# The attention queries of a macaron block as a sixth Strassen group, with queries, keys and values parked in DRAM

## The chip, the core and the metric

The kernel runs on one core of a Trainium2 chip. The metric is the device time of one launch in microseconds, the median of three runs. One further execution was taken with the hardware profiler; all rows below come from it. Engines are named as in the profile: PE (matmuls), PEld (weight loads), DVE (VectorE), ACT (ScalarE), POOL (GpSimd), SP (the queue that starts most loads).

## What is computed

One block on x of 256 tokens by 2048 channels, float32: a half-step SwiGLU feed-forward, then a mixer stage, then a second half-step feed-forward and a last RMSNorm. The mixer stage, which the change touches:

```
h = rmsnorm(x, norm_mix_g)
q_a, k_a, v_a, q_r, k_r, v_r, g_r, gate_a, gate_r = split(h @ w_in)   # widths 1024 x 7, 2048 x 2
att = chunked_band_attention(q_a, k_a, v_a, rel_bias)    # 8 heads of 128, softmax(q k^T + bias) v
ret = silu(g_r) * chunkwise_retention(rotary(q_r), rotary(k_r), v_r)
merged = sigmoid(gate_a) * (att @ w_out_att) + sigmoid(gate_r) * (ret @ w_out_ret)
x = x + merged @ w_out
```

## The kernel before

**Products in three parts.** Every float32 weight chunk of 256 x 512 (KC = 2 blocks of 128 rows) is split into hi and lo: ACT casts it (`hi`, L129), DVE subtracts (`lo`, L130). Each product then takes three matmuls (`three`: hi·hi L140, lo·hi L141, hi·lo L143).

**Steps.** The program is one list of steps, made before anything is issued; `run` walks it. A *standard* step is one chunk against both token tiles: 12 matmuls. A *Strassen group* takes two column blocks of 512 and both token tiles and makes seven half-size products where plain multiplication has eight. It is 28 substeps of 6 matmuls in four phases: phase 0, 1 and 2 have eight each (four r, four s, written 0 to 3), phase 3 has four s. Four "kept" chunks k and four x chunks of the group live in SBUF through the phases. Phase 0 adds k to x (`first`, L532, a DVE add). Phase 1 adds the raw chunk to x (L594), and `third` makes k = x - k (L580) and starts an accumulating DMA on x from POOL (L581). For the chunks named in `added`, the add of phase 0 is an accumulating DMA too (`add_on`, L547), which POOL starts once x has landed; the feed-forwards use `ADDED = (2, 3)`, the gates of the mixers before use none.

**Where standard steps go.** `weave` makes the mixer list: 8 standard steps first (MIX_LEAD), then the groups, with standard steps set between pairs of substeps by a credit that MIX_SHARE gives per pair (four pairs in each of the phases 0 to 2, four single substeps in phase 3). Before, the groups are four gate pairs (`gates`, sigmoid) and the retention gate (silu), five in all, named by their first step: z392, z430, z467, z505, z543. Seven standard jobs of eight steps are woven in: qa0, qa1, ka0, ka1, va0, va1, vr0. `mixed` is the step where the list of groups ends; then come vr1, qr0, kr0, qr1, kr1 as standard jobs (40 steps), and the merge from `mixed + 40`.

**How far engines run ahead.** `prep_upto(c + 4)` splits up to four chunks ahead of the step on PE (SPLIT_BUFS = 4). Raw chunks come by SP's queue through five buffers (RAW_BUFS). k and x of the next group come by POOL's queue, eight at a time (KEPT); where `weave` gets `extra`, ten. All large tiles share one pool of 30 (ACT_TILES). Work called with `later(n, fn)` is issued n steps on, behind the splits of that step, so it stands in line on each engine.

**Attention.** `att_qk_done` scales a finished q or k block, PE transposes it, ACT and DVE copy one half each into a tile (`to_transposed`, L842, L844). From `mixed + 4` on, each head takes five stages, offsets 0, 1, 2, 4, 6 (scores, exp, shares, transposes, values), a new head every four steps. Its PSUM tiles come from a ring of two ("side"), which the transposes of qr and kr and the retention scores also use.

Of the kernel before, what the change touches and what calls it, by code (L numbers as in the profile page):

```python
# [8 lines left out]
F32 = mybir.dt.float32  # L9
F32R = mybir.dt.float32r  # L10
AF = mybir.ActivationFunctionType
# [4 lines left out]
P = 128  # L16
SEQ = 256
NT = SEQ // P
# [3 lines left out]
HEADS = 8  # L22
# [4 lines left out]
NB = 512  # L27
# [7 lines left out]
EXTRA = 2  # L35
# [5 lines left out]
MIX_LEAD = 8  # L41
RET_WAIT = (14, 5)
HELD = 6

MIX_SHARE = (0.85,) * 4 + (1.0,) * 4 + (0.8,) + (0.4,) * 3 + (0.15,) * 4
SHARE = (0.75,) * 4 + (1.0,) * 4 + (0.0,) * 4 + (0.2,) * 4
ADDED = (2, 3)
PLAIN = 10
# [27 lines left out]
def block_kernel(ctx: ExitStack, tc: tile.TileContext, x, g1, w1g, w1u, w1d, gm, w_in, rel, woa, wor, wo,  # L76
                 g2, w2g, w2u, w2d, gf, cos, sin, decay, ident, out):
    nc = tc.nc
# [8 lines left out]
    dram = ctx.enter_context(tc.tile_pool(name="dram", bufs=1, space=bass.MemoryType.DRAM))  # L87

    def act_tile(dt, name):
        return apool.tile([P, 4, SEQ], dt, tag="act", name=name)  # L90
# [7 lines left out]
    def tmp_tile(name, tag="t", bufs=None):  # L98
        return tmp.tile([P, NB], F32, tag=tag, name=name, bufs=bufs)


    steps = []
# [6 lines left out]
    def later(n, fn):  # L109
        due.setdefault(state["step"] + n, []).append(fn)  # L110
# [109 lines left out]
    def add(jobs):  # L220
        for job in jobs:
            for k in range(0, job.nk, KC):
                steps.append(standard(job, k))
# [83 lines left out]
    table = {}  # L307
# [507 lines left out]
    nm = Norm("nm", gains[:, 1, :], True)  # L815
# [11 lines left out]
    QA, KA, VA, QR, KR, VR, GR, GA, GG = 0, W, 2 * W, 3 * W, 4 * W, 5 * W, 6 * W, 7 * W, 7 * W + D  # L827
    scale = HD ** -0.5
    tposed, nat = {}, {}

    def heads_t(ts):
        return slice(ts * P, (ts + 1) * P)

    def to_transposed(key, b, srcs, steps):

        dst = act_tile(F32, f"{key}{b}T")
        tposed[key, b] = dst

        def go(t):
            ps = transpose4(srcs[t], f"{key}{b}p{t}").rearrange("p (i q) -> p i q", i=4)  # L840
            if t == 0:
                nc.scalar.copy(dst[:, :, heads_t(t)], ps)  # L842
            else:
                nc.vector.tensor_copy(dst[:, :, heads_t(t)], ps)  # L844

        for t in range(NT):
            later(steps[t], lambda t=t: go(t))

    def att_qk_done(key, b):
        def done(acc):  # L850
            srcs = []
            for t in range(NT):
                s = tmp_tile(f"{key}{b}{t}", "qk", 4)
                nc.scalar.activation(s, acc[t], AF.Copy, scale=nm.scale(t))
                srcs.append(s)
            to_transposed(key, b, srcs, (2, 2))

        return done
# [32 lines left out]
    def nat_done(key, b, func, after=None):  # L891
        def done(acc):
            dst = act_tile(F32, f"{key}{b}")
            nat[key, b] = dst.rearrange("p a q -> p (a q)").rearrange("p (t n) -> p t n", t=NT)
            for t in range(NT):
                nc.scalar.activation(nat[key, b][:, t, :], acc[t], func, scale=nm.scale(t))
            if after is not None:
                after()

        return done  # L900
# [63 lines left out]
    def all_attention():  # L964
        for h in range(HEADS):
            for s, stage in attention(h):
                later(2 + 4 * h + s, stage)

    def retention(b):

# [53 lines left out]
    w_in0 = w_in[0]  # L1024

    def proj(col, done, tags=("acc", "z")):
        return Gemm(w_in0, 0, col, D // P, nm, done, tags)
# [8 lines left out]
    def gates(col1, col2, func, dsts):  # L1036


        def evict(t, side, r):
            if side == 1:  # L1040
                nc.scalar.activation(r, r, func)
            else:
                bank, r = r, tmp_tile(f"sg{col1}{t}", "gate", 2)
                nc.scalar.activation(r, bank, func, scale=nm.scale(t))
            nc.scalar.dma_start(dsts[side][:, t, :], r)

        return Strassen(nm, w_in0, col1, w_in0, col2, evict)

    both = ("acc", "acc")
    groups = {  # L1050
        b: (lambda b=b: gates(GA + b * NB, GG + b * NB, AF.Sigmoid, merge_dram[b])) for b in range(D // NB)
    }
    groups["gr"] = lambda: gates(GR, GR + NB, AF.Silu, ret_dram)
    weave(
        [proj(QA + b * NB, att_qk_done("qa", b), both) for b in range(2)]
        + [proj(KA + b * NB, att_qk_done("ka", b), both) for b in range(2)]
        + [proj(VA + b * NB, nat_done("va", b, AF.Copy), both) for b in range(2)]
        + [proj(VR, nat_done("vr", 0, AF.Copy), both)],
        0, groups, MIX_LEAD, MIX_SHARE,
    )  # L1060
    mixed = len(steps)
    add([proj(VR + NB, nat_done("vr", 1, AF.Copy))])
    for b in range(2):
        add([proj(QR + b * NB, ret_qk_done("qr", b)), proj(KR + b * NB, ret_qk_done("kr", b, lambda b=b: retention(b)))])

# [79 lines left out]
    def at(step, fn):  # L1145
        due.setdefault(step, []).append(fn)
# [52 lines left out]
    at(mix - 18, load_rel)  # L1199
    at(mix - 18, lambda: later(4, load_gain(gm, 1)))  # L1200
    at(mixed - 4, set_bias)
    at(mixed + 2, all_attention)
    at(merges[0][0] + 4, lambda: later(8, load_gain(g2, 2)))
    at(mixed + 16, load_ret_gates)
    at(mixed + 20, set_decay)
# [66 lines left out]
```

## Time and profile before

| | us |
|---|---|
| median of three runs | 2061.39 (2060.89 to 2062.56) |
| the profiled execution | 2061.97 |
| its span (first to last instruction) | 2060.1 |
| PE busy | 2037.8, 99% of the span |
| DVE busy | 1766.2, 86% |
| ACT busy | 1494.1, 73% |

The span is what the profiler sees; the run's time is 1.9 us longer. The list of all idle time on PE comes to some 22 us, about 5 us of which is the start. The first feed-forward takes the span to about 680, the mixer groups stand from about 708 to 1050, attention and retention to about 1160, the merge to about 1370, the second feed-forward to the end. Busy time of an engine is given by the instructions' own durations; on DVE these overlap a little where one starts before the other has drained.

### The profile page before, as it was taken

What the parts mean: (1) busy time and instruction counts of PE and PEld (TensorE: products, weight loads), DVE (VectorE), ACT (ScalarE), POOL (GpSimd) and SP (SyncE); (2) the same over time, 40 slices, a digit from 0 to 9 for tenths busy, and PEclk for the clock granted to TensorE, in tenths of its full rate; (3) what the DMA queues carried; (4) which work ended last, traced back from release to release, by engine and by line L of the source; (5) the groups of instructions that cost most, each with busy time, mean ns of one, the idle gap of its engine ahead of it and who ended that gap; (6) DMA issues with size and microseconds to landing.
All of it is one profiled execution on the core that took longest, in us unless ns stands there. A gap on an engine that the chain in (4) does not pass through costs nothing.

```text
span 2060.1 us, 26318 instructions
## 1 busy us (share of the span) xinstructions
PE 2037.8 (99%) x9208; PEld 1685.6 (82%) x9208; DVE 1766.2 (86%) x1836; ACT 1494.1 (73%) x1892; POOL 344.8 (17%) x386
## 2 busy tenths in 40 slices
PE   9999999999999999999999999999999999999998
PEld 7888888888888888888888888888888888888886
DVE  7999999999999799889966667569989999989996
ACT  8778877887877767776765434556788888887875
POOL 2221222221222110121100000012122212112200
PEclk9999999999999999999999999999999999999999
DMA  9888899888888677898786645578889888889983
GB/s 308 252 232 260 252 274 273 254 229 252 254 250 244 241 206 262 263 288 240 228 277 184 216 142 189 185 231 218 267 267 278 255 255 234 269 261 268 276 214 133
DMA packets 230325, 498.47 MB, mean 242 GB/s; under 512 B 15584, under 2 KB 16336, under 8 KB 230192
## 3 DMA queue, kind: packets, MB, share of 16 engines
q1 hardware_dynamic: 156736, 301.50, 43.5%
q0 software_dynamic: 70112, 189.44, 36.0%
q10 hardware_dynamic: 3344, 5.84, 0.8%
q8 instruction: 72, 1.18, 0.2%
q14 instruction: 61, 0.50, 0.1%
HBM read 487.81 MB, written 8.91 MB: 241 GB/s over the span
## 4 chain that ended last, share of the span: by engine, by line
PE 92%; ACT 3%; DVE 3%; issue 1%; DMA 1%; DVEq 0%; ACTq 0%; POOLq 0%; POOL 0%
PE acc L143 15%; PE acc L140 15%; PE acc L141 15%; DVE lo L130 1%; DMA raw<-in_w_in_dram 1%; ACT hi L129 0%; PE z392a L143 0%; PE z873a L140 0%; PE z910a L141 0%; PE z765a L141 0%; PE z543a L143 0%; PE z430a L143 0%; PE z801a L143 0%; PE z392a L141 0%; PE z505a L143 0%
## 5 line engine op out<-in xcount | busy, mean ns | idle before, releaser
L130 DVE TENSOR_TENSOR lo<-raw,hi 128x1024 fp32r<-128x1024 f32 x367 | 447.1, 1221 | 142.6 <-ACT hi L129 140.8
L129 ACT CAST hi<-raw 128x1024 fp32r<-128x1024 f32 x367 | 384.3, 1051 | 173.3 <-PE acc L141 138.0
L794 ACT ACTIVATE xall<-acc 128x512 f32<-128x512 f32 x160 | 94.5, 591 | 14.5 <-PE acc L143 10.3
L791 ACT ACTIVATE acc<-xall 128x512 f32<-128x512 f32 x160 | 95.8, 599 | 8.2 <-DVE f1g L758 4.3
L140 PE MATMUL acc<-hi,mgh 128*128 128x512 f32 x128 | 50.2, 392 | 0.0
L141 PE MATMUL acc<-hi,mgl 128*128 128x512 f32 x128 | 49.8, 389 | 0.0
L140 PE MATMUL acc<-hi,nma01h 128*128 128x512 f32 x96 | 38.8, 404 | 0.1
L140 PE MATMUL acc<-hi,nma00h 128*128 128x512 f32 x96 | 38.6, 402 | 0.0
L141 PE MATMUL acc<-hi,nma00l 128*128 128x512 f32 x96 | 37.5, 390 | 0.0
L141 PE MATMUL acc<-hi,nma01l 128*128 128x512 f32 x96 | 37.5, 390 | 0.0
L140 PE MATMUL acc<-hi,nma10h 128*128 128x512 f32 x96 | 37.5, 390 | 0.0
L141 PE MATMUL acc<-hi,nma11l 128*128 128x512 f32 x96 | 37.4, 390 | 0.0
L140 PE MATMUL acc<-hi,nma11h 128*128 128x512 f32 x96 | 37.4, 390 | 0.0
L141 PE MATMUL acc<-hi,nma10l 128*128 128x512 f32 x96 | 37.4, 390 | 0.0
L143 PE MATMUL acc<-lo,mgh 128*128 128x512 f32 x128 | 35.5, 389 | 0.0
L143 PE MATMUL acc<-lo,nma01h 128*128 128x512 f32 x96 | 29.6, 390 | 0.0
L143 PE MATMUL acc<-lo,nma11h 128*128 128x512 f32 x96 | 29.6, 389 | 0.0
L143 PE MATMUL acc<-lo,nma00h 128*128 128x512 f32 x96 | 29.6, 389 | 0.0
L143 PE MATMUL acc<-lo,nma10h 128*128 128x512 f32 x96 | 29.6, 389 | 0.0
L143 PEld LDWEIGHTS acc<-lo,mgh 128*128 128x128 f32 x128 | 24.0, 188 | 5.0
L141 PEld LDWEIGHTS acc<-hi,mgl 128*128 128x128 f32 x128 | 24.0, 188 | 4.9
L140 PEld LDWEIGHTS acc<-hi,mgh 128*128 128x128 f32 x128 | 24.0, 188 | 4.8
(6634 smaller groups left out, 7134.3 us busy)
## 6 DMA issues: line engine op xcount, KB each, us to landing
raw<-in_ffn_w_down_dram SPq DMA_DIRECT2D x176, 512.0 KB, 7.6
raw<-in_w_in_dram SPq DMA_DIRECT2D x96, 512.0 KB, 4.7
raw<-in_w_out_dram SPq DMA_DIRECT2D x32, 512.0 KB, 4.1
raw<-in_ffn_w_up_dram SPq DMA_DIRECT2D x16, 512.0 KB, 6.4
raw<-in_w_out_att_dram SPq DMA_DIRECT2D x16, 512.0 KB, 4.3
raw<-in_w_out_ret_dram SPq DMA_DIRECT2D x16, 512.0 KB, 3.9
raw<-in_ffn_w_gate_dram SPq DMA_DIRECT2D x15, 512.0 KB, 4.8
z392x<-in_w_in_dram POOLq DMA_DIRECT2D x8, 512.0 KB, 7.5
```

Of the source, the lines that this page charges most:

```text
L129: nc.scalar.copy(hi, raw)
L130: nc.vector.tensor_sub(lo, raw, hi.bitcast(F32))
L140: nc.tensor.matmul(acc, ahi, whi, start=first, stop=False, **more)
L141: nc.tensor.matmul(acc, alo, whi, start=False, stop=False, **more)
L143: nc.tensor.matmul(acc, ahi, wlo, start=False, stop=last, **more)
L791: nc.scalar.activation(acc, xs[t][:, cols], AF.Copy, scale=2.0)
L794: nc.scalar.activation(xs[t][:, cols], acc, AF.Copy, scale=0.5)
```

## The change

1. The queries (qa0 and qa1, sixteen standard steps) become a Strassen group, the first of six (`queries`). Its results are transposed one step after they appear.
2. All six groups of the mixers use `ADDED`, and `weave` gets `EXTRA` (ten kept chunks after the first group).
3. vr1 moves from behind `mixed` into the woven jobs (now ka0, ka1, va0, va1, vr0, vr1), so 32 steps lie between `mixed` and the merge.
4. MIX_SHARE gives phase 0 less, phase 2 only its last step, phase 3 a little.
5. Queries, keys and values are written to DRAM when done, from ACT's queue (`put_away`), and read back by POOL around `mixed` (`bring_back`).
6. Heads start at `mixed` + 3, 6, 10, 13, 17, 20, 24, 27 rather than every four steps from `mixed + 4`.

```diff
+HEAD_AT = (3, 6, 10, 13, 17, 20, 24, 27)
-MIX_SHARE = (0.85,) * 4 + (1.0,) * 4 + (0.8,) + (0.4,) * 3 + (0.15,) * 4
+MIX_SHARE = (0.5,) * 4 + (1.0,) * 4 + (0.0,) * 4 + (0.2,) * 4
...
+    to_dram = {key: [dram.tile([P, 4, SEQ], F32, name=f"{key}{b}d") for b in range(HEADS // 4)] for key in ("qa", "ka", "va")}
+    def put_away(table, key, b, tile):
+        nc.scalar.dma_start(to_dram[key][b], tile)
+        del table[key, b]
+    def bring_back(b):
+        for table, key in ((tposed, "qa"), (tposed, "ka"), (nat, "va")):
+            t = act_tile(F32, f"{key}{b}back")
+            nc.gpsimd.dma_start(t, to_dram[key][b])
+            table[key, b] = t if table is tposed else by_tokens(t)
...
+        if home is not None:
+            later(max(steps) + 1, lambda: put_away(tposed, key, b, dst))
...
-                later(2 + 4 * h + s, stage)
+                later(HEAD_AT[h] + s, stage)
...
-        return Strassen(nm, w_in0, col1, w_in0, col2, evict)
+        return Strassen(nm, w_in0, col1, w_in0, col2, evict, ADDED)
...
+    def queries():
+        srcs = [{}, {}]
+        def evict(t, side, r):
+            if side == 0:
+                bank, r = r, tmp_tile(f"qa0{t}", "gate", 2)
+                nc.scalar.activation(r, bank, AF.Copy, scale=nm.scale(t))
+            srcs[side][t] = r
+            if len(srcs[side]) == NT:
+                to_transposed("qa", side, srcs[side], (1, 1))
+        return Strassen(nm, w_in0, QA, w_in0, QA + NB, evict, ADDED)
+    groups = {"qa": queries, **groups}
     weave(
-        [proj(QA + b * NB, att_qk_done("qa", b), both) for b in range(2)]
-        + [proj(KA + b * NB, att_qk_done("ka", b), both) for b in range(2)]
+        [proj(KA + b * NB, att_qk_done("ka", b), both) for b in range(2)]
         + [proj(VA + b * NB, nat_done("va", b, AF.Copy), both) for b in range(2)]
-        + [proj(VR, nat_done("vr", 0, AF.Copy), both)],
-        0, groups, MIX_LEAD, MIX_SHARE,
+        + [proj(VR + b * NB, nat_done("vr", b, AF.Copy), both) for b in range(2)],
+        0, groups, MIX_LEAD, MIX_SHARE, None, EXTRA,
     )
-    add([proj(VR + NB, nat_done("vr", 1, AF.Copy))])
...
+    at(mixed - 3, lambda: bring_back(0))
+    at(mixed + 5, lambda: bring_back(1))
-    at(mixed + 2, all_attention)
+    at(mixed, all_attention)
```

The groups are now z392 (queries), z427, z462, z496, z531, z566.

On POOL, where a new group's chunks k and x are fetched in the middle of the mixers. Before, the third group's:

```order
L543 DMA z467k2_7421<-in_w_in_dram 128x2x512 [waits DMASW3_49,DVE_49]
L543 DMA z467x2_7433<-in_w_in_dram 128x2x512 [waits DMASW4_49,DVE_49]
L543 DMA z467k3_7450<-in_w_in_dram 128x2x512 [waits DMASW5_49,DVE_49]
L543 DMA z467x3_7468<-in_w_in_dram 128x2x512 [waits DMASW6_49,DVE_49]
L581 DMA z467x0_7355<-in_w_in_dram 128x2x512 [waits DMASW7_49,DVE_49,Activation_49]
```

And now:

```order
L544 DMA z462k2_7292<-in_w_in_dram 128x2x512 [waits DMAHW7_49,DMASW7_49]
L544 DMA z462x2_7304<-in_w_in_dram 128x2x512 [waits DMAHW1_49,DMASW0_49]
L544 DMA z462k3_7328<-in_w_in_dram 128x2x512 [waits DMASW1_49,DVE_49]
L544 DMA z462x3_7340<-in_w_in_dram 128x2x512 [waits DMASW2_49,DVE_49]
L548 DMA z462x2_7304<-in_w_in_dram 128x2x512 [waits DMASW3_49,DMASW0_49]
L548 DMA z462x3_7340<-in_w_in_dram 128x2x512 [waits DMASW4_49,DMASW2_49]
L544 DMA z496k0_7359<-in_w_in_dram 128x2x512 [waits DMASW5_49,DVE_49]
L544 DMA z496x0_7377<-in_w_in_dram 128x2x512 [waits DMASW6_49,DVE_49]
L582 DMA z462x0_6941<-in_w_in_dram 128x2x512 [waits DMASW7_49,DVE_49,Activation_49]
```

Two accumulating transfers (L548), each waiting for its chunk to land, have come in behind x3, and the next group's first two chunks have moved ahead of the phase 1 accumulates.

On ACT, at the first group's end, around the copy of the transposed qa1 (`hi` names are the casts that PE's next substeps need). Now:

```order
L858 COPY qa1T_6884<-qa1p0_6896 128x4x128 [waits DMASW6_49,PE_49]
L130 CAST hiz42700s_6914<-z427x0_6762 128x1024 [waits DVE_49,PE_49,Activation_49]
L834 DMA qa1d_97<-qa1T_6884 128x1024 [waits DVE_49,Activation_49]
L130 CAST hiz42702r_6925<-z427k2_6822 128x1024 [waits DMASW1_49,PE_49]
L1081 ACTIVATE qa01_6929<-z392a_6426,nmrstd_91 128x512 [waits PE_49]
```

Before, after the same copy:

```order
L842 COPY qa1T_6805<-qa1p0_6824 128x4x128 [waits PE_49]
L129 CAST hiz39222s_6842<-z392k2_6319 128x1024 [waits DVE_49,PE_49]
L129 CAST hiz39223s_6854<-z392k3_6364 128x1024 [waits DVE_49,PE_49]
L129 CAST hi425_6866<-raw425_6728 128x1024 [waits DMAHW1_49,DVE_49,PE_49]
L129 CAST hiz39230s_6886<-z392x0_6228 128x1024 [waits DMASW7_49,DVE_49,PE_49]
```

A write to DRAM that waits for DVE's half of the copy has come in between two casts, and the copy itself has moved from phase 2 to the next group's phase 0.

## Rows read from the trace of the kernel before

**Rows 1.** The page's busy times by engine; then all recorded waits of PE:

```profile
PE 2037.8 (99%) x9208; PEld 1685.6 (82%) x9208; DVE 1766.2 (86%) x1836; ACT 1494.1 (73%) x1892; POOL 344.8 (17%) x386
...
PE acc L143 <- DVE lo L130: 4.9, 9, 0.6
...
PE kr0p L385 <- DVE attl L380: 0.6, 1, 0.6
```

**Rows 2.** Busy time by stretch (feed-forward, mixers): engines' sums, clock, DMA share, GB/s:

```profile
120.00:640.00 520.00, 515.70 (x2298) 424.97 (x2297) 477.62 (x439) 416.36 (x509) 111.62 (x119) 1.00 0.87 252
720.00:1040.00 320.00, 319.87 (x1428) 264.96 (x1427) 291.10 (x264) 223.22 (x242) 49.23 (x54) 1.00 0.81 252
```

**Rows 3.** Chain of work, last matmuls of standard steps: start us, us, what:

```profile
711.20 0.91 PE acc L143 x4
...
713.92 0.91 PE acc L143 x4
```

**Rows 4.** Timeline of PE, first matmul of two substeps: start us, us, engine, line:

```profile
850.65 0.39 PE L140 MATMUL z430a<-hiz43030s,nma11h 128*128 128x512 f32 x1
...
852.01 0.39 PE L140 MATMUL z430a<-hiz43031s,nma11h 128*128 128x512 f32 x1
```

**Rows 5.** Timeline of DVE at full pace, start of a group (start to start):

```profile
852.29 0.68 DVE L654 TENSOR_TENSOR z430c<-z430c,z430s 128x512 f32<-128x512 f32 x1
852.89 1.22 DVE L130 TENSOR_TENSOR loz46700r<-z467k,hiz46700r 128x1024 fp32r<-128x1024 f32 x1
854.03 1.22 DVE L532 TENSOR_TENSOR z467x<-z467x,z467k 128x1024 f32<-128x1024 f32 x1
855.19 1.22 DVE L130 TENSOR_TENSOR loz46701r<-z467k,hiz46701r 128x1024 fp32r<-128x1024 f32 x1
```

**Rows 6.** Timelines: DVE makes a lo part, PE takes it; two places in the mixers:

```profile
794.27 1.22 DVE L130 TENSOR_TENSOR loz43000s<-z430x,hiz43000s 128x1024 fp32r<-128x1024 f32 x1
...
796.26 0.62 PE L143 MATMUL z430c<-loz43000s,nms5h 128*128 128x512 f32 x2
...
1020.58 1.22 DVE L130 TENSOR_TENSOR loz54313s<-z543x,hiz54313s 128x1024 fp32r<-128x1024 f32 x1
...
1022.88 0.62 PE L143 MATMUL z543a<-loz54313s,nms6h 128*128 128x512 f32 x2
```

**Rows 7.** The page's DMA queues: packets, MB, share of the span of 16 engines:

```profile
q1 hardware_dynamic: 156736, 301.50, 43.5%
q0 software_dynamic: 70112, 189.44, 36.0%
q10 hardware_dynamic: 3344, 5.84, 0.8%
```

**Rows 8.** Stretches of 5 us in the mixers, columns as in Rows 2:

```profile
895.00:900.00 5.00, 5.00 (x23) 4.14 (x23) 5.00 (x6) 3.74 (x4) 1.67 (x4) 1.00 1.10 226
905.00:910.00 5.00, 4.87 (x22) 3.69 (x21) 1.78 (x2) 2.15 (x3) 0.00 (x0) 1.00 1.04 397
```

**Rows 9.** Feed-forward: POOL's fetches for z154, the cast that ends them; landing times of L547:

```profile
268.15 1.19 POOL L581 DMA_DIRECT2D z118x<-in_ffn_w_up_dram  x1 [1.08 <-DVE z118k L580]
...
275.37 0.72 POOL L543 DMA_DIRECT2D z154x<-in_ffn_w_gate_dram  x1 [2.20 <-DVE loz11821s L130]
...
291.85 1.21 POOL L547 DMA_DIRECT2D z154x<-in_ffn_w_up_dram  x1 [4.15 <-DMA z154x<-in_ffn_w_gate_dram]
...
301.05 1.06 ACT L129 CAST hiz15403s<-z154x 128x1024 fp32r<-128x1024 f32 x1 [0.30 <-PE z154c L141]
...
DMA to landing us min/median/max: 5.8/7.5/9.3
```

**Rows 10.** Timeline of ACT: a cast in the mixers' phase 2 that waited for a raw chunk:

```profile
907.85 1.05 ACT L129 CAST hi<-raw 128x1024 fp32r<-128x1024 f32 x1 [3.40 <-DMA raw<-in_w_in_dram]
```

**Rows 11.** Timelines of POOL and PE: the bias is fetched, and first used:

```profile
1024.20 2.04 POOL L347 DMA_DIRECT2D biasT<-rel_ext  x2
...
1050.53 0.60 PE L358 MATMUL psb<-id_sb,biasT 128*128 128x128 f32 x4
```

More of the change, by code (lines that the diff above doesn't have):

```diff
@@ L829, in block_kernel, with by_tokens @@
     tposed, nat = {}, {}
+    to_dram = {key: [dram.tile([P, 4, SEQ], F32, name=f"{key}{b}d") for b in range(HEADS // 4)] for key in ("qa", "ka", "va")}
[7 more added lines that the diff above has]
+            table[key, b] = t if table is tposed else by_tokens(t)
+    def by_tokens(t):
+        return t.rearrange("p a q -> p (a q)").rearrange("p (t n) -> p t n", t=NT)
     def heads_t(ts):
@@ L837, in to_transposed @@
         tposed[key, b] = dst
+        home = to_dram.get(key)
         def go(t):
@@ L893, in done @@
             dst = act_tile(F32, f"{key}{b}")
-            nat[key, b] = dst.rearrange("p a q -> p (a q)").rearrange("p (t n) -> p t n", t=NT)
+            nat[key, b] = by_tokens(dst)
             for t in range(NT):
                 nc.scalar.activation(nat[key, b][:, t, :], acc[t], func, scale=nm.scale(t))
+            if key in to_dram:
+                put_away(nat, key, b, dst)
             if after is not None:
```

## The prediction

> **What bounds the kernel now.** I read the page's busy times first, then all waits of PE, then stretches by stage, and only then single instructions. PE is busy for 2037.8 us, 99% of the span; DVE has 86% and ACT 73% [rows 1]. The stretch table says that the mixers have no slack on PE at all: 319.87 us busy out of 320, with DVE at 291.1 and the DMA engines at 0.81. A feed-forward stretch looks the same on PE with DVE at 0.92 and DMA at 0.87 [rows 2]. So in the stage that the change touches PE's own work sets the time. Work taken off PE shortens the run one for one; anything that makes PE wait lengthens it one for one; and DVE, DMA and POOL matter only where they run out of slack. The question is thus one subtraction: PE work removed, less new waits.
>
> **Part 1, PE work.** Two query jobs of eight standard steps go. One standard step is the distance between the last matmuls of neighbouring steps, 713.92 - 711.20 = 2.72 us [rows 3], so 16 x 2.72 = 43.5 us. In their place come 28 Strassen substeps, each 852.01 - 850.65 = 1.36 us [rows 4], so 38.1 us. The difference is -5.4 us. Everything else that PE does, transposes included, is only moved. Two smaller waits could vanish with it: 0.6 us before kr0p, and 0.13 us in the stretch 905 to 910 [rows 1, 8]. So the ceiling of the gain is about 6.1 us, and I take 5.44.
>
> **Part 2, DVE.** At full pace one 128 x 1024 operation of DVE follows another after 1.14 us (852.89, 854.03, 855.19), though each is recorded as 1.22; the two evictions ahead of a group take 1.3 us [rows 5]. By the new table of shares the six groups carry 40 standard steps after the lead, 6.7 each (counted by walking the credit of MIX_SHARE; before, 48 in five, 9.6 each). A group then asks of DVE 28 splits, ten adds and subtractions (there were twelve; two `first` adds become DMAs) and 6.7 standard splits: 44.7 x 1.14 + 1.3 = 52.2 us. PE needs 38.1 + 6.7 x 2.72 = 56.3, a surplus of 4.1. Before it was 49.6 x 1.14 + 1.3 = 57.8 against 64.2, a surplus of 6.4. In the mean DVE still keeps up. The worst part is phase 1 with three standard steps in it, 19 operations or 21.6 us against 19.0 on PE: DVE falls back 2.6 us. The four chunks of split lead must carry that, and did before: phase 1 was as dense, and its lo parts came 0.77 and 1.08 us before PE took them (794.27 + 1.22 against 796.26, and 1020.58 + 1.22 against 1022.88) [rows 6]. With less standard work in phase 0 the lead may enter phase 1 a little lower. Bounds 0 to 1 us over all groups; I take 0.3, near the rows that show no wait.
>
> **Part 3, the DMA engines.** From the queue rows I price a chunk in busy time per engine: q1 is 43.5% of 2060.1 = 896 us for 301.5 MB, or 575 chunks of 0.524 MB, 1.56 us each. In the stretch 905 to 910, 1.04 x 5 us moved 397 GB/s x 5 us = 1.985 MB, 3.8 chunks, 1.37 each [rows 7, 8]. POOL's queue has 36.0% = 741.6 us for 200 plain fetches (25 groups of eight), 140 accumulating ones (six in each of the feed-forwards' 20 groups, four in the mixers' five) and some 11 MB besides, which I estimate at 29 us; (741.6 - 200 x 1.37 - 29)/140 = 3.1 us each for an accumulating one. A group of the mixers now asks for 8 x 1.37 + 6 x 3.13 + 14.7 raw x 1.56, some 3.0 for its writes of gates and 1.5 for a share of the put-away tiles (q10's price [rows 7], 2.8 us per MB): 57.2 us in 56.3 us of PE. That is a share of 1.02, where the feed-forwards, which carry the same six accumulating transfers but more standard work per group and no such writes, show 0.87, and the mixers before 0.81 [rows 2]. The greatest 5 us stretch I found has 1.10 [rows 8]. So the cover of all the transfers comes close to its end, and this is where I expect the loss.
>
> Here a rule of the Trainium skill speaks for the change. The rows show an occupied share of 1.10 at only 226 GB/s, while accumulating transfers run, and 1.04 at 397 GB/s [rows 8]. The Trainium skill, "DMA: Bandwidth & Descriptors", section "Where 436 GB/s comes from", has it that for traffic between HBM and SBUF a limit of about 358 GB/s per core binds. By it the new groups' some 16 MB in 56 us, 290 GB/s, would leave a fifth free, nothing would wait, and the time would be that of the first rival below. The rows of 226 GB/s at a full share speak against counting by bytes.
>
> **Part 4, the added transfers' chain.** In a feed-forward group x3 is fetched at 275.37, its second term is started at 291.85, after 4.15 us of waiting for it to land, and the cast that reads it runs at 301.05, 9.2 us later; such a transfer lands 5.8 to 9.3 us after issue [rows 9]. In the mixers one standard step fewer stands ahead of that cast (2.72 us), so 9.2 - 2.72 = 6.5 us remain: -0.7 to 2.8 us late. The writes of gates (some 2.2) and a put-away (1.5) share the engines just then, less one raw chunk (1.56): up to 4.9 late. The four chunks of split lead take up some 2.6 us of it, so PE waits 0 to 2.3 us at a tight transition. Three of the five are tight by the table of shares (into z427, z496 and z531); I take 0.5 each, nearer the rows in which nothing waits, 1.5 in all, with 0 and 6.9 as the ends.
>
> **Part 5, the rest.** On ACT the put-away of qa stands between two casts and waits for DVE's half of the copy, some 1.9 us; behind it queue the next casts, for which PE waits in turn, with 0.77 us of margin nearby [rows 6]: 0 to 0.8 us, I take 0.3. Raw chunks in phase 2: one cast waited 3.40 us for its chunk [rows 10], and PE lost 0.13 us in that stretch [rows 8]; phase 2 now has only one standard step, so the raw chunks of the seconds come faster one after another: 0 to 1, I take 0.2. Heads closer: stages are set at 3 to 4 steps where there were 4, so some now share a step with transposes of qr and kr in a ring of two PSUM tiles; before, this ring cost 0.6 us once [rows 1]. 0 to 2 us, I take 0.5. Reading the tiles back and the bias cost nothing, since POOL is far ahead there: the bias was fetched at 1024.20 and first used at 1050.53, 26 us later [rows 11]; without that cover a read of 0.5 MB would show its whole landing, some 6 to 9 us [rows 9]. Head 7's values now come two steps before the merge rather than five; that still is 5.4 us.
>
> **The sum.** -5.44 + 0.3 + 1.5 + 0.3 + 0.2 + 0.5 = -2.64 us. The profiled execution took 2061.97 us (span 2060.1 and 1.9 outside it), which is 0.6 above the median of the runs, 2061.39; the sum is a difference, so I take it from the median: 2058.8 us. The ends of the unknown terms go from no loss (2055.9, or 2055.3 with the old waits gone) to all losses (0 + 1 + 6.9 + 0.8 + 1 + 2 = 11.7 us, so 2067.7).
>
> **The rivals.**
> Full credit: the chunks' lead swallows all of it, and at most 1.3 us of waits come: 2055.9 to 2057.3. For it speaks that the mixers hardly wait at all before, and that feed-forward groups with the same chain run without loss [rows 1, 2, 9]. Against it, the share of 1.02. Chance 0.36.
> Saturated DMA, slower than before: with transfers asking for more than the engines have, the lateness does not heal within a group and comes back at each of the five transitions, in the phase 0 casts of x2 and x3. It decides from 5.44/5 = 1.1 us a transition, and is slower by 0.2% (4.1 us) from (5.44 + 4.1)/5 = 1.9 us each; 2.3 us each, the end of part 4, gives 2061.39 - 5.44 + 11.5 = 2067.5. For it speaks the sum of 57.2 in 56.3; against it that the sum rests on mean prices, which contain queueing already. Chance 0.24 for 2061.4 to 2068, of which 0.14 beyond 2065.5.
> The forecast, partial give-back: 2057.3 to 2061.4, chance 0.40.
> That the groups do not take the queries over is no rival: the order of the changed kernel has the substeps, and 24 matmuls fewer.
>
> **How the numbers follow.** The forecast is 2058.8. Below 2055.8 I leave some 0.04, above 2065.5 0.14, so the range is 2055.8 to 2065.5. A measurement of this kernel can tell about 0.2%, 4.1 us, from no change: faster than 2057.3 is the first rival, 0.36; slower than 2065.5 is 0.14; the rest, 0.50, is within.
>
> **What would show it.** Right, if PE has 24 matmuls and some 5.4 us of work less, the mixers' stretches show DMA shares near 1.0, and PE's new waits are for casts of x2 and x3 in phase 0 of z427, z496 and z531, each under 2.3 us. The first rival: PE is idle for under 1.3 us more in all. The slower rival: waits at every transition, over 1.1 us. Wrong in another way, if PE waits for ACT behind the put-aways by more than 0.8 us, for lo parts of phase 1 by more than 1, for a tile brought back at all, or between heads by more than 2.

## The result, and the profile after

The changed kernel takes 2064.88 us (median of 20 runs, 2063.03 to 2067.66) against 2061.57 us (20 runs, 2060.64 to 2062.93): a ratio of 1.0017, interval 1.001 to 1.0024. It is 3.3 us slower where 2.6 us less was forecast: within the stated range of 2055.8 to 2065.5, but on the other side of no change. The profiled execution took 2063.38 us, span 2061.6, so it is one of the lighter ones: 1.5 us of span above the profile before.

The work did fall. The page's busy line, to be read beside [rows 1], has 24 matmuls fewer (9208 to 9184):

```profile
PE 2034.4 (99%) x9184; PEld 1677.0 (81%) x9184; DVE 1779.4 (86%) x1850; ACT 1502.6 (73%) x1906; POOL 372.9 (18%) x416
```

The loss is in new waits. From the first substep of z392 to the first n2p transpose, the same work but for the queries, the kernel before takes 582.60 us (725.54 to 1308.14), the changed one 585.11 (724.53 to 1309.64). Less the 5.44 us of removed work it should have been 577.2: some 8 us were lost. All of PE's recorded waits in that stretch (us in total, times, longest); before, there was only the 0.6 of kr0p:

```profile
PE qa0p L386 <- ACT qa L1081: 1.6, 1, 1.6
PE acc L144 <- DVE lo L131: 1.2, 2, 0.6
PE z531c L144 <- DVE loz53113r L131: 0.6, 1, 0.6
PE as L933 <- ACT p L971: 0.6, 1, 0.6
PE z531c L141 <- ACT hiz53103s L130: 0.5, 1, 0.5
PE z462c L144 <- DVE loz46212r L131: 0.2, 1, 0.2
```

These are 4.7 us. A step around such a stop is 0.3 us longer than the stop itself, and some short ones are not recorded. The stretches (columns as in [rows 2]) show where they lie, and that DMA now has 0.94 to 0.96 where it had 0.81:

```profile
780.00:840.00 60.00, 58.35 (x268) 47.65 (x266) 53.34 (x50) 42.47 (x48) 13.18 (x14) 1.00 0.96 285
840.00:900.00 60.00, 59.15 (x260) 48.32 (x259) 54.63 (x49) 42.17 (x47) 14.42 (x15) 1.00 0.95 294
960.00:1020.00 60.00, 58.17 (x251) 46.23 (x250) 52.40 (x47) 40.43 (x45) 14.44 (x15) 1.00 0.94 279
```

**The first loss: a write on ACT.** ACT and then PE at the end of the first group (start, duration, engine, line, operation, in brackets the idle time before and what ended it):

```profile
781.89 1.05 ACT L130 CAST hiz42700s<-z427x 128x1024 fp32r<-128x1024 f32 x1 [0.76 <-PE z392a L142]
784.92 0.33 ACTq L834 DMA_DIRECT2D qa1d<-qa1T  x1
...
785.35 1.04 ACT L130 CAST hiz42702r<-z427k 128x1024 fp32r<-128x1024 f32 x1 [2.41 <-PE z427a L144]
786.30 0.68 ACT L1081 ACTIVATE qa<-z392a,nmrstd 128x512 f32<-128x512 f32 x1
```

```profile
784.83 0.60 PE L386 MATMUL qa0p<-id_sb,qa 128*128 128x128 f32 x4
787.04 0.66 PE L386 MATMUL qa0p<-id_sb,qa 128*128 128x128 f32 x4 [1.61 <-ACT qa L1081]
```

The put-away of qa1 stands in ACT's line and waits for DVE's half of the copy, until 784.55. ACT does nothing from 782.94 to 784.92. Behind it waits not only a cast, but the scaling of the second half of qa0, which PE is to transpose one step later. PE stops for 1.6 us in the record, and the step is 2.0 us too long. The row names PE as the releaser of the cast at 785.35; the write above it shows what held ACT.

**The second loss: x3 comes late, and the price is paid a phase later.** ACT, DVE and then PE in z531:

```profile
966.73 1.05 ACT L130 CAST hiz53102s<-z531x 128x1024 fp32r<-128x1024 f32 x1 [3.01 <-DMA z531x<-in_w_in_dram]
970.30 1.05 ACT L130 CAST hiz53103s<-z531x 128x1024 fp32r<-128x1024 f32 x1 [2.52 <-DMA z531x<-in_w_in_dram]
```

```profile
967.82 1.23 DVE L131 TENSOR_TENSOR loz53102s<-z531x,hiz53102s 128x1024 fp32r<-128x1024 f32 x1 [2.15 <-ACT hiz53102s L130]
971.38 1.22 DVE L131 TENSOR_TENSOR loz53103s<-z531x,hiz53103s 128x1024 fp32r<-128x1024 f32 x1 [2.33 <-ACT hiz53103s L130]
```

```profile
987.56 0.73 PE L144 MATMUL z531c<-loz53113r,nms3h 128*128 128x512 f32 x2 [0.62 <-DVE loz53113r L131]
...
995.51 0.73 PE L144 MATMUL acc<-lo,nma01h 128*128 128x512 f32 x2 [0.62 <-DVE lo L131]
```

DVE stood 4.5 us in phase 0, waiting for casts that waited for a transfer. PE lost 1.1 us there (0.5 of it is recorded as a wait). The rest of its loss came 16 to 24 us later, in phase 1, where DVE has more to do than PE and no transfer is waited for: a reader of PE's waits alone sees only "DVE lo" and would blame DVE. Summed over all brackets from 780 to 1075, DVE stood 14.9 us for casts of x2 and x3.

Why x3 is late is on POOL:

```profile
957.57 1.23 POOL L548 DMA_DIRECT2D z531x<-in_w_in_dram  x1 [12.51 <-DMA z531x<-in_w_in_dram]
962.42 1.22 POOL L548 DMA_DIRECT2D z531x<-in_w_in_dram  x1 [3.62 <-DMA z531x<-in_w_in_dram]
```

The second term of x3 is started at 962.42 and cast at 970.30, 7.9 us later, where the feed-forward had 9.2 [rows 9]; it had to wait for x2 and x3 to land. These are the fourth and the last of six fetches started from 937.85 to 944.34.

### The profile page after: what moved, and what is told of

Read it like the earlier page. It is cut to its first block, busy times and chain, and to the rows that moved or that the text cites. A ratio compares the mean times of both kernels' runs of the same rounds, so it can differ in the third digit from the quotient of the medians.

```text
span 2061.6 us, 26378 instructions
## 1 busy us (share of the span) xinstructions
PE 2034.4 (99%) x9184; PEld 1677.0 (81%) x9184; DVE 1779.4 (86%) x1850; ACT 1502.6 (73%) x1906; POOL 372.9 (18%) x416
## 4 chain that ended last, share of the span: by engine, by line
PE 88%; DVE 3%; ACT 3%; issue 3%; DMA 3%; POOL 1%; DVEq 0%; SPq 0%; ACTq 0%; POOLq 0%
PE acc L144 15%; PE acc L142 14%; PE acc L141 14%; DMA z531x<-in_w_in_dram 1%; DVE lo L131 1%; DMA z994k<-in_ffn_w_up_dram 1%; DMA z462x<-in_w_in_dram 0%; PE z885a L142 0%; PE z813a L144 0%; PE z704a L144 0%; PE z922a L142 0%; PE z566a L142 0%; PE z777a L144 0%; PE z849a L141 0%; PE z885a L141 0%
## 5 line engine op out<-in xcount | busy, mean ns | idle before, releaser
L131 DVE TENSOR_TENSOR lo<-raw,hi 128x1024 fp32r<-128x1024 f32 x351 | 426.8, 1219 | 124.6 <-ACT hi L130 121.4
L130 ACT CAST hi<-raw 128x1024 fp32r<-128x1024 f32 x351 | 367.2, 1050 | 157.3 <-PE acc L142 124.8
L795 ACT ACTIVATE xall<-acc 128x512 f32<-128x512 f32 x160 | 94.5, 591 | 14.6 <-PE acc L144 10.3
L141 PE MATMUL acc<-hi,nma01h 128*128 128x512 f32 x80 | 32.5, 406 | 0.0
L141 PE MATMUL acc<-hi,nma00h 128*128 128x512 f32 x80 | 32.3, 404 | 0.0
L142 PE MATMUL acc<-hi,nma01l 128*128 128x512 f32 x80 | 31.3, 391 | 0.0
L142 PE MATMUL acc<-hi,nma11l 128*128 128x512 f32 x80 | 31.2, 391 | 0.0
L142 PE MATMUL acc<-hi,nma00l 128*128 128x512 f32 x80 | 31.2, 390 | 0.0
L141 PE MATMUL acc<-hi,nma11h 128*128 128x512 f32 x80 | 31.2, 390 | 0.0
L141 PE MATMUL acc<-hi,nma10h 128*128 128x512 f32 x80 | 31.2, 390 | 0.0
L141 PE MATMUL acc<-hi,atth 128*128 128x512 f32 x64 | 26.2, 410 | 0.0
```

The source lines that it names most:

```text
L130: nc.scalar.copy(hi, raw)
L131: nc.vector.tensor_sub(lo, raw, hi.bitcast(F32))
L141: nc.tensor.matmul(acc, ahi, whi, start=first, stop=False, **more)
L142: nc.tensor.matmul(acc, alo, whi, start=False, stop=False, **more)
L795: nc.scalar.activation(xs[t][:, cols], acc, AF.Copy, scale=0.5)
```

## The experiments

The ratio compares each kernel with the kernel before on the same chip, whose median there was 2061.1 to 2061.5 us (2061.57 for the changed kernel); with 4 to 11 runs each, medians less than some 2 us apart are not told apart by the intervals. The profiles give three stretches that all kernels share: A, from the first substep of z392 to that of z462 (two groups); B, from there to the first bias transpose (four groups); C, from there to the first n2p.

| kernel | A us | B us | C us | median us | ratio to before |
|---|---|---|---|---|---|
| changed | 120.4 | 228.7 | 236.0 | 2064.88 | 1.0017 (1.001 to 1.0024) |
| e1 | 119.7 | 229.6 | 236.3 | 2065.22 | 1.0019 (1.001 to 1.0028) |
| e2 | 121.0 | 225.2 | 236.7 | 2061.77 | 1.0002 (0.9993 to 1.0011) |
| e3 | 120.2 | 229.0 | 236.0 | 2065.51 | 1.0019 (1.001 to 1.0028) |
| e4 | 138.2 | 224.0 | 236.1 | 2077.96 | 1.0079 (1.0066 to 1.0093) |
| e5 | 119.8 | 224.0 | 236.1 | 2059.73 | 0.9992 (0.9983 to 1.0001) |
| e6 | 120.5 | 224.0 | 236.1 | 2059.06 | 0.999 (0.9981 to 0.9999) |
| e7 | 119.4 | 224.0 | 236.1 | 2059.28 | 0.999 (0.9981 to 0.9999) |
| e8 | 118.8 | 227.6 | 236.2 | 2070.24 | 1.0045 (1.0032 to 1.0059) |
| e9 | 119.1 | 224.0 | 236.1 | 2058.41 | 0.9984 (0.9976 to 0.9993) |
| e10 | 119.1 | 225.5 | 236.1 | 2059.70 | 0.9993 (0.9984 to 1.0002) |
| e11 | 125.0 | 225.6 | 241.6 | 2070.72 | 1.0045 (1.0033 to 1.0058) |
| e12 | 119.1 | 224.0 | 236.1 | 2058.31 | 0.9984 (0.9975 to 0.9993) |

**e1: the put-aways three steps later.**

```diff
-            later(max(steps) + 1, lambda: put_away(tposed, key, b, dst))
+            later(max(steps) + 4, lambda: put_away(tposed, key, b, dst))
```

> The changed kernel, with the put-aways of queries and keys issued three steps later; nothing else differs. In the changed kernel's trace ACT stood from 782.94 to 784.92 for the put-away of qa1, which waits for DVE's half of the copy, and PE then lost 2.0 us at qa0p, whose source ACT had not yet scaled. Theory (the waiting put-away held ACT up): the stop before qa0p goes, and the time falls by 1.7 to 2.0 us. Rival (ACT and DVE are late there anyway, since a new group begins): PE stops at the next cast or lo part instead, and the time falls by less than 0.7 us.

The stop is gone, all eight transposes of qa0 stand in one row of PE:

```profile
786.17 1.03 PE L386 MATMUL qa0p<-id_sb,qa 128*128 128x128 f32 x8
```

But the time is the same (2065.2). In this profile z427 stops twice in phase 1 (1.5 us), and x2 and x3 of z531 came later still, as ACT and then PE show:

```profile
967.77 1.05 ACT L130 CAST hiz53102s<-z531x 128x1024 fp32r<-128x1024 f32 x1 [3.98 <-DMA z531x<-in_w_in_dram]
971.83 1.04 ACT L130 CAST hiz53103s<-z531x 128x1024 fp32r<-128x1024 f32 x1 [3.01 <-DMA z531x<-in_w_in_dram]
```

```profile
972.93 0.50 PE L141 MATMUL z531c<-hiz53103s,nms5h 128*128 128x512 f32 x1 [1.95 <-ACT hiz53103s L130]
```

This stop of 1.95 us cost more than itself. Behind it PE's granted clock (the column before the last two) was 0.50, that is 1.2 GHz, and then again 1.00, 2.4 GHz:

```profile
974.00:976.00 2.00, 2.00 (x6) 1.49 (x5) 1.95 (x3) 2.00 (x3) 0.00 (x0) 0.50 0.00 0
977.00:980.00 3.00, 3.00 (x15) 2.45 (x14) 3.00 (x4) 1.90 (x3) 0.00 (x0) 1.00 0.79 220
```

From 973.50 to 976.91 eight matmuls followed each other after 0.43 us in place of 0.23, 1.6 us in all. In the changed kernel PE's stops in the mixers were 1.6 us at most and the clock stayed at 1.00.

So the write was the cause of that stop, but taking it away gained nothing while transfers are late behind it. The rival's number came out, for another reason than the rival gave (see e10).

**e2: no accumulating second terms in phase 0 of the mixers.**

```diff
-        return Strassen(nm, w_in0, col1, w_in0, col2, evict, ADDED)
+        return Strassen(nm, w_in0, col1, w_in0, col2, evict)
-        return Strassen(nm, w_in0, QA, w_in0, QA + NB, evict, ADDED)
+        return Strassen(nm, w_in0, QA, w_in0, QA + NB, evict)
```

> The changed kernel with the mixers' added set empty: the two accumulating transfers a group that start in phase 0 become two adds on DVE, as before. Some 12 transfers of 512 KB less DVE-free, and 2 x 1.14 us more on DVE a group. Theory (the late second term of x2 and x3 empties the lead of splits in phase 0, and phase 1, where DVE has more to do than PE, then makes PE wait): ACT's waits of 2 to 3 us for x3 go, PE's waits in z462 and z531 (about 5 of the 7.9 us lost in the stage) go for the greater part, time down by 2 to 4 us. Rival (phase 1 is simply too dense for DVE, whatever comes before): the waits stay or grow, since DVE has 52.2 + 2.3 = 54.5 us in 56.3, time the same or up by 1 to 3 us.

3.1 us less, B 3.5 us shorter, although DVE does two more operations a group. DVE's idle time for casts of x2 and x3 is 0.6 us in place of 14.9. Phase 1 has the same work as in the changed kernel, and PE's waits for lo parts from z392 to n2p fall from 2.0 us in four to 1.0 in two. The two largest rows of PE's waits there:

```profile
PE qa0p L386 <- ACT qa L1081: 1.6, 1, 1.6
PE acc L144 <- DVE lo L131: 1.0, 2, 0.6
```

The theory holds; that phase 1 is too dense whatever comes before does not. The edit also takes twelve transfers away (the DMA share from z392 to the first bias transpose is 0.85, in the changed kernel 0.94), so it does not tell a late transfer from too many; e5 does.

**e3: one standard step from phase 1 to phase 0.**

```diff
-MIX_SHARE = (0.5,) * 4 + (1.0,) * 4 + (0.0,) * 4 + (0.2,) * 4
+MIX_SHARE = (1.0,) * 4 + (0.5,) * 4 + (0.0,) * 4 + (0.2,) * 4
```

> The changed kernel with the shares of phase 0 and 1 exchanged (1.0 and 0.5): one standard step a group moves from phase 1 to phase 0. The cast of x3 is due 2.72 us later; phase 1 has 2.72 us less PE work but only 1.14 us less DVE work, so it is denser on DVE by 1.6 us. Theory of the late second term: ACT's waits for x3 (2.0 to 2.7 us a group) go, and with a full lead phase 1 costs 0 to 1 us: time down by 2 to 4 us. Rival (phase 1 too dense for DVE): PE's waits in phase 1 grow in all six groups, by up to 1.6 us each: time up by 3 to 9 us.

No change (2065.5), which neither side had forecast. ACT's wait for x3 of z531 fell from 2.52 to 1.12 us, but a stop of about 0.9 us remained in phase 1 of each of z462, its successor and z531, each time behind four to six substeps with no standard step between them. And the last group lost the standard step between its phases 2 and 3, where PE then waited for an eviction:

```profile
1069.05 0.50 PE L141 MATMUL z566a<-hiz56630s,nma11h 128*128 128x512 f32 x1 [1.64 <-ACT z566c L652]
```

It shows that DVE's deficit in phase 1 is real (19 operations, as the prediction counted it): standard steps there are what covers it. Both sides had a part, and the run does not weigh them.

**e4: x2 and x3 first.** All mixer groups fetch x2, x3, then k0, x0, k1, x1, k2, k3, and start the second terms right behind x3.

```diff
...
+            if self.w[0] is w_in0:
+                out = [out[i] for i in (5, 7, 0, 1, 2, 3, 4, 6)]
+                out[1] = lambda x3=out[1]: [x3(), add_on()]
+            else:
+                out[-1] = lambda last=out[-1]: [last(), add_on()]
-            out[-1] = lambda last=out[-1]: [last(), add_on()]
```

> The changed kernel with the mixers' chunks fetched in another order: x2 and x3 first and their second terms started right behind, then k0, x0, k1, x1, k2, k3. With the two extra kept chunks this starts the second terms of z462, z496, z531 and z566 some 40 us earlier; the work of DVE and ACT is the same, and so are the transfers. Theory of the late second term: ACT's waits for x3 and the PE waits that follow in z462 to z566 go, time down by 3 to 4.5 us. Rival (phase 1 too dense for DVE): no change within 0.7 us. Second rival (the DMA engines have too much in all, 1.02 by the estimate): the lateness moves to k0 and x0, and PE waits at the group's start, by 1 to 3 us each; time the same or longer. z427 has no extra chunks, so its k0 may come late in either case, 0 to 3 us.

The whole got 13 us longer, the four later groups 4.7 us shorter (B, 228.7 to 224.0). All the loss is in the first two groups, which have no extra chunks (A is 17.8 us longer; the expectation allowed for 0 to 3 in z427): there k0 and x0 stand on POOL behind the second terms, which wait for x2 and x3 to land. So in these two groups the lateness moved to k0 and x0, as the second rival has it, but by the order on POOL; in the four others the theory holds. All PE waits from 720 to 850:

```profile
PE ka0p L387 <- ACT ka L877: 4.2, 1, 4.2
PE qa0p L387 <- ACT qa L1086: 3.8, 1, 3.8
PE z427a L142 <- ACT hiz42700r L131: 3.0, 1, 3.0
PE z392a L142 <- ACT hiz39200r L131: 1.4, 1, 1.4
PE qa0p L387 <- ACT qa1T L863: 0.7, 1, 0.7
```

**e5: the same order, from the third group on.**

```diff
-            loads = group.loads()
+            loads = group.loads(n > 1 and share is MIX_SHARE)
...
-            out[-1] = lambda last=out[-1]: [last(), add_on()]
+            if early:
+                out = [out[i] for i in (5, 7, 0, 1, 2, 3, 4, 6)]
+            i = 1 if early else -1
+            out[i] = lambda x3=out[i]: [x3(), add_on()]
```

> The changed kernel with x2 and x3 fetched first, and their second terms started right behind, in the four groups that have the extra kept chunks (z462, z496, z531, z566); the first two groups keep their order. In the last kernel, where all six had the new order, the stretch from the first substep of z462 to the first bias transpose took 224.0 us, and 228.7 in the changed kernel; what it lost lay in the first two groups. Theory of the late second term: the stretch takes 224 to 225 us, the first two groups are as in the changed kernel, time down by 3.5 to 5 us against it, to 2060 to 2061.5. Rival (the gain belonged to the shifted phase of transfers behind late first groups): less than 1.5 us.

5.2 us less than the changed kernel. The same work and the same transfers, in another order. POOL starts the second term for z496 at 848.56, before z462 is in its phase 1 (the changed kernel: 898.44), and ACT takes x2 and x3 of z531 without any wait for a DMA:

```profile
848.56 1.23 POOL L548 DMA_DIRECT2D z496x<-in_w_in_dram  x1 [14.46 <-DMA z496x<-in_w_in_dram]
```

```profile
961.81 1.06 ACT L130 CAST hiz53102s<-z531x 128x1024 fp32r<-128x1024 f32 x1
964.08 1.06 ACT L130 CAST hiz53103s<-z531x 128x1024 fp32r<-128x1024 f32 x1 [1.21 <-PE acc L142]
```

And from 840 to 900 the DMA engines are fuller than in the changed kernel (1.00, there 0.95) while PE loses nothing:

```profile
840.00:900.00 60.00, 60.00 (x267) 49.67 (x266) 56.41 (x51) 44.21 (x49) 13.07 (x14) 1.00 1.00 304
```

So a share of 1.0 over 60 us was not what cost time; when the awaited transfer was started was. For the stretch from 780 to 840 (1.04) this run does not show it: z427, which has no extra chunks, lies there, and in e6, which differs in the put-aways alone, ACT waited 3.1 us for its x3. e9 shows it for that stretch too.

**e6 and e7: put-aways later on top of e5, and the new order in the feed-forwards on top of e6** (`group.loads(n > 1)`).

> The last kernel with the put-aways of queries and keys three steps later as well. Alone, that took the stop of 2.0 us before qa0p away, but 1.5 us came back as waits for lo parts in phase 1 of z427, and the time was the same. Theory (z427 has no slack after its late x2 and x3, so the 2.0 us only move): time within 0.7 us of the last kernel. Rival (the two losses are independent): 1.5 to 2 us less than the last kernel.

> The last kernel with the new order of fetches also in both feed-forwards, from each one's third group on. There the second term of x3 is cast 9.2 us after it is started, and lands 5.8 to 9.3 us after. Theory: PE's waits for lo parts in the feed-forwards (6.2 us in all recorded, others hidden in 515.6 of 520 us) fall by 1 to 4 us. Rival (these waits come with standard steps that follow each other, not with x2 and x3): no change within 0.7 us.

e6 is the same as e5, as the theory has it (the median 0.7 us lower, A in the profile 0.7 longer): the stop before qa0p is gone, and z427 lost 2.2 us in its place, in three places from 798 to 815. e7 is the same as e6, and PE's waits for lo parts in the first feed-forward are 5.1 us in both: they do not come from x2 and x3.

**e8: no writes of queries, keys and values in the mixers.**

```diff
-        nc.scalar.dma_start(to_dram[key][b], tile)
         del table[key, b]
...
+    at(60, fill)
```

> The changed kernel without the writes of queries, keys and values to DRAM in the mixers: their places in DRAM are filled with weights during the first feed-forward instead, and read back as before, so the attention works on other numbers. 3.1 MB of writes go, some 9 us of busy time on each DMA engine by the price of q10, and ACT has no waits for them. Theory of the late second term by its chain of issue (x3 is fetched and started too late, whatever the load): the stop before qa0p goes, and the waits in z462 and z531 stay, time down by 0 to 2 us. Rival (a saturated DMA: every transfer delays x3): the waits in z427, z462 and z531, where the put-aways lie, fall by more than half, time down by 3 to 5 us.

The first feed-forward, where the filling stands in POOL's line, is 9.6 us longer (z392 begins at 734.12, not 724.53), so the time as a whole tells nothing. From z392 to n2p the kernel is 2.6 us shorter than the changed one. A is 1.6 us shorter, and z531 still waits:

```profile
PE acc L144 <- DVE lo L131: 1.2, 2, 0.6
PE z531c L144 <- DVE loz53113r L131: 0.6, 1, 0.6
```

B is 1.1 us shorter of the 4.7 that e5 gained. But x2 and x3 were not less late: ACT's waits for them from z427 to z566 come to 16.8 us, against 11.4 in the changed kernel's profile and 18.7 in e1's. So the rival fails: the traffic of the put-aways is not what makes x2 and x3 late. Where B's 1.1 us come from is not shown.

**e9 and e10: second terms on DVE where there are no extra chunks.** e9 is e6 with `added` empty for the queries and the first gate pair; e10 is e2 with the later put-aways of e1.

> The kernel e6 (early x2 and x3 in the last four groups, put-aways later) with the second terms of the first two groups, z392 and z427, added on DVE again, since these two have no extra chunks and so cannot start the transfers earlier. In e6 the waits that were left in the mixers were 2.2 us in z427 (0.48 in phase 0, 0.81 and 0.92 in phase 1) and 0.9 in z531. Theory (z427 loses by its late x2 and x3 too): these 2.2 us fall to under 0.8, time 1.4 to 2 us below e6's 2059.1. Rival (z427 is short of DVE because the transposed copies of queries and keys lie in it): two more adds there make the waits 0 to 2 us longer.

> The kernel e2 (no accumulating second terms in phase 0 of the mixers) with the put-aways of queries and keys three steps later. In e2 the largest stop left was the one before qa0p, 2.2 us. With the second terms on DVE z427 does not wait for DMA. If the 2.0 us of e1 came back as waits because z427 had its x3 late, they stay gone here: 1.5 to 2.2 us below e2's 2061.8. If they came back because DVE and ACT are short there in any case: within 0.7 us of e2.

e9 takes 2058.41 us, 3.1 less than the kernel before (0.9984, 0.9976 to 0.9993). z427 has no stop left, as the theory has it. Against e6 that is 0.7 us by the medians, 1.0 less by each one's own kernel before and 1.4 in A; the theory's 1.4 to 2 us are at the edge of what the runs can tell. All of PE's waits from z392 to n2p:

```profile
PE acc L144 <- DVE lo L131: 0.6, 1, 0.6
PE as L936 <- ACT p L974: 0.6, 1, 0.6
```

Here two stretches with a share about 1.0 stand beside a PE that never stops:

```profile
780.00:840.00 60.00, 60.00 (x278) 49.72 (x277) 57.76 (x55) 43.90 (x50) 13.10 (x14) 1.00 1.01 309
900.00:960.00 60.00, 60.00 (x267) 49.69 (x266) 55.70 (x50) 44.75 (x49) 13.07 (x14) 1.00 1.00 307
```

e10 is 2.1 us under e2, and A is 1.9 us shorter: with no late transfer in z427, the later put-away gives its 2 us. This bears out the reading of e1.

**e11: a lead of five chunks in the mixers.**

```diff
-SPLIT_BUFS = 4
+SPLIT_BUFS = 5
-ACT_TILES = 30
+ACT_TILES = 28
...
+    at(mix, lambda: room.update(ahead=SPLIT_BUFS))
+    at(mixed, lambda: room.update(ahead=4))
```

> The changed kernel with five slots for split chunks in place of four, used as a lead of five chunks in the mixers alone (four elsewhere); to make room the pool of large tiles has 28 in place of 30. Theory (one cushion of four chunks was asked to cover both the late x3 of phase 0 and DVE's deficit of phase 1): a chunk more of lead, 1.4 to 2.7 us of PE work, takes the waits in z462 and z531 (5 us) down by half or more, time down by 2 to 4 us, unless the fetches, with two tiles fewer, come later in their turn. Rival (x3 and everything behind it are late by as much as they are early in lead, since an earlier cast needs an earlier transfer): waits for x3 stay the same on PE's side, no change within 0.7 us.

B is 3.1 us shorter, as the theory has it, although ACT waits no less for x2 and x3 in these four groups (13.8 us, 10.3 in the changed kernel): more lead takes up the late x3. But A is 4.6 us longer and C 5.6:

```profile
PE ka1p L386 <- ACT ka L872: 3.7, 1, 3.7
PE psb L359 <- ACT bias L365: 2.9, 1, 2.9
```

In A the scaling of ka stood in ACT's line behind the casts of x2 and x3 of z427, which now come a chunk sooner and waited 3.63 and 3.54 us for their transfers; in C the copy of the bias stood behind two casts that waited 3.32 and 2.38 us for raw chunks. Behind both stops the granted clock was 0.50 (from 801 to 803 and from 1086 to 1089). How much the two missing tiles add is not shown.

**e12: the third head one step earlier**, on e9: `HEAD_AT = (3, 6, 9, 13, 17, 20, 24, 27)`.

> The kernel e9 with the third head one step earlier (mixed + 9 in place of 10), so that its scores no longer share a step with the second head's transposes and qr0p; nothing else moves. In all kernels with the closer heads PE stopped there, 0.57 us of recorded wait of the scores for ACT's copy of the second head's transposes, 0.89 and 0.41 us over the nominal pace in all, where a pair without a stop has 0.16 and 0.23. Theory (the ring of two tiles): the stop goes, the stretch from the first bias transpose to the first n2p is 0.7 to 0.9 us shorter than e9's 236.1, time 0 to 1 us under e9's 2058.4. Rival (the copy on ACT is late whatever asks for it): the stop moves to the values of the first head or to qr0p, stretch within 0.2 us.

C is the same to 0.1 us. The stop of `as` is gone, and the second head's transposes (`apt`) wait for DVE's att part, with longer steps beside it:

```profile
PE apt L972 <- DVE attl L381: 0.3, 1, 0.3
```

So the stop only moves; the rival is right in that, though not in the place it named.

## Why the prediction failed

**What bounds the kernel** was right: in the changed kernel PE's time in the mixers moved by its own work and its waits. In e1, e4 and e11, where stops were longer, a lower clock behind them came on top.

**Part 1** was right in size as far as the count goes (24 matmuls). e9 shows what can be had of it: 579.2 us from z392 to n2p against 582.6, 3.4 of the 5.4.

**Parts 2 and 4 failed together**, and this is the main error: 0.3 and 1.5 us stood for what cost 4.7 us in the profile (B of the changed kernel less B of e5: 1.5 in z462, 0.6 in z496, 2.6 in z531), with some 1.3 in A on top (against e9, the put-away's stop included). Each was priced alone against the four chunks of split lead, which were to take up some 2.6 us in the one and some 2.6 us in the other. But phase 0 and phase 1 follow each other in the same group: what the late x3 takes out of the lead in phase 0 is missing when DVE falls 2.6 us behind in phase 1. The size of the lateness was forecast within its bounds for x3 alone (up to 4.9 us; ACT waited 1.1 to 2.7 for it in z427, z462, z496 and z531), but not for x2 and x3 together, which made 5.5 us in z531. The deficit of phase 1 was counted rightly. The rows of [rows 6] were no evidence that the lead carries it: the first, `loz43000s`, is a lo part of phase 0 and not of phase 1, and the second comes from a group in which no x2 or x3 had been late. The measured 4.7 us lie between the 1.8 taken and the ends, 1 + 6.9. And z462, which lost 1.5, was not among the three transitions called tight.

**Part 3**: the share came to 0.94 to 0.96, not 1.02. The price of an accumulating transfer holds: the added POOL traffic is 806.1 - 741.6 = 64.5 us in the queue row below, and less eight plain fetches and six reads at 1.37 it leaves some 45 us for 16 accumulating ones, 2.8 each (an estimate; the prediction's was 3.1).

```profile
q0 software_dynamic: 76480, 205.17, 39.1%
```

But what was drawn from it, that a full share is itself the danger, is refuted by e9: 1.01 and 1.00 over 60 us each, with PE busy for all of them. The prediction weighed a rule of the Trainium skill here ("DMA: Bandwidth & Descriptors", section "Where 436 GB/s comes from"), that about 358 GB/s bind between HBM and SBUF. By it nothing was saturated, and at 307 and 309 GB/s e9 shows no wait; but [rows 8] had 397 GB/s over 5 us, more than that limit, so here it does not bind. Full credit failed all the same, since the loss was one of order.

**Part 5**: the put-away was set at 0.3 us, bound 0.8, and stopped PE for 2.0. The mechanism was the right one; the bound was taken from the margin of a lo part (that of `loz43000s`, 0.77), while the next in ACT's line was the scaling of qa0, with PE due one step behind it. Heads closer were set at 0.5 and cost 0.2: C is 236.0 us, where the kernel before less vr1's eight steps has 257.6 - 21.8 = 235.8; the stop before kr0p (0.6) is gone, one before `as` (0.6) has come. For raw chunks in phase 2 and for tiles brought back PE has no recorded wait.

**The slower rival** named the right wait, casts of x2 and x3 at the transitions, but the wrong cause (a saturated DMA) and the wrong place on PE: of the 4.7 us of recorded waits only 0.5 are for such a cast in phase 0. The time fell into its band, 2061.4 to 2068, for another reason than it gave.

**Open**: the median lies 3.3 us above before, the profile 1.5. Of the difference 1.0 us lies ahead of the mixers, in code that the change does not touch (z392 begins at 725.54 before and at 724.53 now). One part is seen at the start, where PE stops for 2.2 us in both profiles and its granted clock is 0.50 behind the stop in the kernel before, 1.00 in the changed one (first row before, second row changed):

```profile
48.00:51.00 3.00, 3.00 (x9) 2.32 (x8) 2.44 (x4) 2.57 (x4) 0.00 (x0) 0.50 0.23 42
48.00:51.00 3.00, 3.00 (x15) 2.49 (x14) 3.00 (x4) 2.57 (x4) 0.00 (x0) 1.00 0.04 7
```

The runs of the changed kernel spread over 4.6 us, those of e9 over 1.6, and the waits for x2 and x3 of z531 were 5.5 us in one profile and 7.0 in e1's; that late transfers vary from run to run, and that a longer stop brings a lower clock with it, is the likely reason, but it was not measured over runs. Of the 2.1 us that e9 misses of the 5.44, 1.8 lie before the first bias transpose: 0.9 are the stop in z531, some 0.7 short stops in phase 0 of z392, neither of them removed.

## What to carry over

- A lead of finished work is one cushion. Before two possible delays are priced as covered, ask whether they fall within one refill of it; if they do, add them first and subtract the cushion once.
- When PE waits for DVE, look one phase back for DVE's own idle time: the engine named in the wait was short of time because something had kept it idle some 20 us before. And where a fetch has a second, dependent part, put it first in its queue, if there is room to hold it; the same transfers in another order were worth 5.2 us here.
- A DMA that is issued from a computing engine waits in that engine's line for its data, and so does a cast that waits for a transfer: a wait of 2 us on ACT became 2 us on PE (the put-away), one of 3.5 us became 3.7 (e11). Put such work some steps after its data are due. Whether that gains time depends on what is late next: nothing in e1, 2 us in e10.

## What the runs showed of the hardware

- DMA engines at a share of 1.01 and 1.00 over two stretches of 60 us, at 309 and 307 GB/s, stood beside a PE that was busy for all 60 us of each (e9). Over these stretches the share told how full the engines were, not that PE would wait.
- A chunk that is accumulated keeps the DMA engines busy for 2.8 to 3.1 us of the mean engine, a plain one for 1.4 to 1.6 (estimates from the queue rows).
- PE's granted clock was 0.50 (1.2 GHz) for some 3 us behind a stop of 1.95 us (e1, z531) and behind stops of 3.7 and 2.9 us (e11). Behind the stop of 1.6 us before qa0p it was 1.00 (changed kernel), and behind one of 2.2 us once 0.50 and once 1.00 (the start of the kernel before and of the changed one).
